# Reordering the weight chunks of a gated linear recurrence, with its decay work cut into steps

## The chip, the cores and the metric

The kernel runs on one core of a Trainium2 chip. The metric is the device time of one execution in microseconds (us). It is a forward pass of a four-layer network over 256 tokens of width 1024 in one launch; the change touches one stage of it, some 140 us long, in the middle of the third layer.

## The reference, cut to what matters

The stage is the mixer of the third layer, a chunked linear recurrence with a forget gate. One product `u @ w_in` gives four groups of 1024 columns: query, forget gate, value and output gate, each for 8 heads of 128.

```python
q_raw, f_raw, v, g = proj[:, :, 0], proj[:, :, 1], proj[:, :, 2], proj[:, :, 3]
log_f = jnp.log(lb + (1.0 - lb) * jax.nn.sigmoid(f_raw))
k = (1.0 - lb) * jax.nn.sigmoid(-f_raw)
q = jax.nn.silu(q_raw)
...
b = jnp.cumsum(log_f, axis=2)                 # within a chunk of tokens
q_dec = q * jnp.exp(b)
k_inv = k * jnp.exp(-b)
...                                           # scores, values, state from chunk to chunk
o = o * lax.rsqrt(jnp.mean(o * o, axis=-1, keepdims=True) + NORM_EPS)
o = o * norm_g.astype(jnp.float32).reshape(H, HG_VDIM)
o = o.reshape(B, S, D_MODEL) * jax.nn.silu(g.reshape(B, S, D_MODEL))
return o.astype(u.dtype) @ w_out
```

## The kernel before, in words

All products with weights are computed from operands that are split into a high and a low part, three products for each. A chunk of weights is 1024 x 256: one DMA of 1 MB into `raw`; ScalarE writes the high part `whi` in two halves of 128 x 1024; VectorE writes the low part `wlo` of the first half. In this stage GpSimd writes the low part of the second half (`pool_lo`). A chunk is then 48 matmuls of 256 columns on TensorE. There are buffers for the split parts of two chunks, so the parts of a chunk are written while the chunk before it is multiplied, and over those of the chunk before that: the first half becomes free when three quarters of that earlier chunk are done, the second half at its end.

The order on TensorE is the order in which the program is written (`manual_schedule` for it alone). ScalarE, VectorE and GpSimd work through orders that a planner sets when the kernel is built: each takes, of what is ready by the planner's own estimates, the instruction that the program names first. On the chip these orders are fixed, and each engine waits for the next instruction in its own order.

The stage, `hgrn`, has 17 chunks of products. Value and gate of head pair 0 come first, together. Then the four forget chunks follow each other; each is followed on ScalarE by an exponential (`he`), and on VectorE by an addition (`hs`), a reciprocal, a product (`kk`) and two scalings (`lf`). When all four are done, ScalarE takes the logarithm of `lf` in one instruction (`self.act(f2, f2, AF.Ln)`), VectorE makes eight scans (`bt`) and one difference (`rl`), ScalarE makes the exponentials of +`rl` and -`rl`, and VectorE makes eight products for `kk`. The rest are the chunks of the four head pairs: query 0; value 1, query 1, gate 1; value 2, query 2, gate 2; value 3, query 3, gate 3.

A head pair's own work, `hgrn_pair`, is a generator. `tick()` advances every generator in the background list by one step, and is called twice in each chunk (once in each of the four groups of 12 matmuls of the output projection that use the first half of the heads). Its steps are: a first empty one (five for pair 0), transposes of `kk` (`phk`), scores (`pha`), chunk states (`phs`, then `hS` on VectorE, a chain of three states), outputs (`pho`) with the normalisation after them (squares `hjunk` on ScalarE, `hss` on VectorE, a power `hF` on GpSimd, `hsg` on VectorE), an empty one, and the transposes `pot` into the operand (`hoh`, `hol`) of the output projection. `settle()` ticks until the named generators have ended. The output projection (`out_proj`, tile `po`) settles everything before its first matmuls with the second half of the heads.

Of the kernel before, what the change touches and what calls it, by code (L numbers as in the profile page):

```python
# [7 lines left out]
F32 = mybir.dt.float32  # L8
# [3 lines left out]
AF = mybir.ActivationFunctionType  # L12
OP = mybir.AluOpType
# [5 lines left out]
KT = 8  # L19
# [71 lines left out]
class Net:  # L91
# [1280 lines left out]
    def hgrn(self, nxt):  # L1372
        nc, tc, i = self.nc, self.tc, self.i
        w = self.w3(i["hgrn_w_in"][0])
        lb, ilb = self.lb, self.ilb
        v3 = lambda x: x.rearrange("p (k t) -> p k t", t=T)
        u, tile = self.next
        self.hold = True
        with self.phase("hgrn", 6) as hp:
            G = self.bcast_row(hp, "G", self.grow[0][0])  # L1380
            self.hmask = hp.tile([128, 128], I32, name="hmask")
            nc.sync.dma_start(self.hmask, i["hmask"])
            reset = hp.tile([128, 256], F32, name="reset")
            nc.sync.dma_start(reset, i["cst3"][:, 64:320])
            out = self.pair("ho")
            v, sg = {}, {}
            c = slice(0, 256)
            pv, pg = self.toks([w[:, :, 2048:3072][:, :, c], w[:, :, 3072:4096][:, :, c]], u, ["phv", "phg"], tile)
            self.hgrn_v(0, v, pv, hp)
            self.hgrn_g(0, sg, pg, hp)  # L1390
            self.pool_lo = True
            kk, lf = v3(self.A("kk")), v3(self.A("lf"))
            for p in range(4):
                ps = self.ws(w[:, :, 1024 + 256 * p:1024 + 256 * (p + 1)], u, "pf")
                e = hp.tile([128, 512], F32, tag="he", name="he", bufs=2)
                s = hp.tile([128, 512], F32, tag="hs", name="hs", bufs=2)
                self.act(e, ps, AF.Exp, scale=-1.0)
                self.ts(s, e, 1.0, None, OP.add)
                nc.vector.reciprocal(s, s)
                self.tt(kk[:, 2 * p:2 * p + 2, :].rearrange("p a b -> p (a b)"), e, s, OP.mult)  # L1400
                for b in range(2):
                    k = 2 * p + b
                    self.ts(lf[:, k, :], s[:, b * T:(b + 1) * T], ilb[:, k:k + 1], lb[:, k:k + 1], OP.mult, OP.add)
            f2 = lf.rearrange("p k t -> p (k t)")
            self.act(f2, f2, AF.Ln)
            bt, rl = self.A("bt"), self.A("rl")
            b3 = v3(bt)
            for k in range(KT):
                nc.vector.tensor_tensor_scan(b3[:, k, :], reset, lf[:, k, :], 0.0, op0=OP.mult, op1=OP.add)
            bc = bt.rearrange("p (c t) -> p c t", t=64)  # L1410
            rc = rl.rearrange("p (c t) -> p c t", t=64)
            self.tt(rc, bc, bc[:, :, 31:32].to_broadcast([128, 32, 64]), OP.subtract)
            E = [hp.tile([128, 8, 3], F32, tag=f"hE{n}", name=f"hE{n}") for n in range(2)]
            self.act(E[0], rl.rearrange("p (k c t) -> p k c t", c=4, t=64)[:, :, 0:3, 63], AF.Exp)
            self.act(E[1], bt.rearrange("p (k c t) -> p k c t", c=4, t=64)[:, :, 1:4, 31], AF.Exp)
            ep = bt
            self.act(f2, rl, AF.Exp, scale=-1.0)
            self.act(ep, rl, AF.Exp)
            for k in range(KT):
                self.stt(kk[:, k, :], kk[:, k, :], ilb[:, k:k + 1], lf[:, k, :])  # L1420
            am = []
            for n in range(2):
                a = hp.tile([128, 4, 128], F32, tag=f"am{n}", name=f"am{n}")
                nc.vector.memset(a, 0.0)
                am.append(a)
            ch = []
            for p in range(4):
                c = slice(256 * p, 256 * (p + 1))
                if p:
                    self.hgrn_v(p, v, self.tok(w[:, :, 2048:3072][:, :, c], u, "phv"), hp)  # L1430
                ps = self.ws(w[:, :, c], u, "phq")
                if p > 1:
                    self.settle(ch[p - 2])
                q = hp.tile([128, 2, T], F32, tag="hq", name="hq", bufs=2)
                q2 = q.rearrange("p a b -> p (a b)")
                self.silu2(q2, ps)
                self.stt(q2, q2, 0.5, v3(ep)[:, 2 * p:2 * p + 2, :].rearrange("p a b -> p (a b)"))
                ch.append(self.hgrn_pair(p, q, v, sg, kk, E, am[p % 2], hp, out))
                self.bg.append(ch[p])
                if p:  # L1440
                    self.hgrn_g(p, sg, self.tok(w[:, :, 3072:4096][:, :, c], u, "phg"), hp)
            self.pool_lo = False
            self.hold = False
            a = self.as_act(*out)
            self.out_norm(self.w3(i["hgrn_w_out"][0]), a, G, nxt)

    def hgrn_v(self, p, v, pv, hp):
        v[p] = hp.tile([128, 2, 2, 128], F32, tag="hv", name="hv", bufs=2)
        self.act(v[p].rearrange("p t h d -> p (t h d)"), pv)

    def hgrn_g(self, p, sg, pg, hp):
        sg[p] = hp.tile([128, 2, 2, 128], F32, tag="hsg", name="hsg", bufs=2)
        self.silu2(sg[p].rearrange("p t h d -> p (t h d)"), pg)

    def hgrn_pair(self, p, q, v, sg, kk, E, am, hp, out):
        nc = self.nc
        H = 2 * p
        v = v[p]
        for _ in range(1 if p else 5):
            yield  # L1460
        pk = self.pss("phk")
        for t in range(2):
            for h in range(2):
# [19 lines left out]
        for n in range(3):  # L1483
# [3 lines left out]
            t, o = n // 2, 64 * (n % 2)  # L1487
# [14 lines left out]
        for t in range(2):  # L1502
            for h in range(2):
                n = 2 * t + h
# [360 lines left out]
```

## Time and profile before

| | us |
|---|---|
| median of 3 runs | 2248.33 |
| lowest, highest | 2245.28, 2248.53 |
| the profiled execution | 2249.15 |
| its span, first to last instruction | 2247.3 |

The span is divided by engine: PE is TensorE's matmuls, PEld its weight loads, DVE VectorE, ACT ScalarE, POOL GpSimd, SP the queue that issues the DMAs. A busy PE isn't PE at its peak, and an idle engine that nothing waits for costs nothing. The stage of the change lies from about 1411 us (norm and first two chunks) to 1567 us of the span; its forget chunks begin at 1428.9 us.

### The profile page before, as it was taken

To read this page: it belongs to the slowest core of one execution; us is meant where nothing else is said; L and a number is where in the kernel's file an instruction comes from. 1 tells how busy PE (TensorE), PEld (TensorE's weight loads), DVE (VectorE), ACT (ScalarE), POOL (GpSimd) and SP (SyncE) were. 2 spreads that over 40 slices of the span, in tenths; PEclk is the share of its full clock that TensorE was granted. 3 is DMA by queue.
4 is the path that set the end of the run, shared out by engine and by line. 5 is a ranking of instruction groups with operands and counts; after the bars stand their busy time and mean duration, and the time that the engine had idled before them with its cause. 6 is when DMAs were issued, how large, how long until landed. Compare 5 with 4: busy or idle time off the path is not lost.

```text
span 2247.3 us, 38710 instructions
## 1 busy us (share of the span) xinstructions
PE 2171.4 (97%) x15635; PEld 2006.1 (89%) x15635; DVE 1683.8 (75%) x2596; ACT 1273.6 (57%) x1992; POOL 163.8 (7%) x142
## 2 busy tenths in 40 slices
PE   8999999999999999999999998989999999999998
PEld 7998998998899999788888886887998899998997
DVE  6879677776587886599999996777787676665554
ACT  5655545445566554487877775655543555555443
POOL 0031100000003210000000000331000000000000
PEclk9999999999999999999999999999999999999999
DMA  7444577876454366689999994434687554444553
GB/s 239 150 134 145 195 243 246 276 267 233 158 169 141 117 224 209 219 311 356 335 317 349 321 345 156 156 121 160 209 290 282 184 183 147 154 150 136 182 181 131
DMA packets 338527, 478.61 MB, mean 213 GB/s; under 512 B 9874, under 2 KB 239116, under 8 KB 338340
## 3 DMA queue, kind: packets, MB, share of 16 engines
q1 hardware_dynamic: 338340, 476.05, 62.7%
q8 instruction: 125, 2.05, 0.4%
q14 instruction: 62, 0.51, 0.1%
HBM read 474.95 MB, written 1.06 MB: 212 GB/s over the span
## 4 chain that ended last, share of the span: by engine, by line
issue 31%; PE 23%; DVE 2%; POOL 1%; ACT 1%; POOLq 0%; DVEq 0%; ACTq 0%
PE peg L176 5%; PE peu L176 5%; PE pey L176 5%; PE pf L176 1%; PE po L176 1%; PE phg L176 1%; DVE wlo L164 1%; PE phq L176 1%; PE pgat L176 1%; PE phv L176 1%; PE pho L176 1%; PE psc L176 0%; PE pht L179 0%; POOL ms L351 0%; POOL rs L182 0%
## 5 line engine op out<-in xcount | busy, mean ns | idle before, releaser
L164 DVE TENSOR_TENSOR wlo<-raw,whi 128x1024 fp32r<-128x1024 f32 (+2 forms) x802 | 930.1, 1180 | 289.2 <-ACT whi L161 281.4
L161 ACT ACTIVATE whi<-raw 128x1024 fp32r<-128x1024 f32 (+3 forms) x828 | 832.3, 1023 | 508.9 <-PE po L176 60.3
L176 PE MATMUL pu<-uh,whi 128*128 128x256 f32 x480 | 134.1, 279 | 0.0
L176 PE MATMUL pg<-uh,whi 128*128 128x256 f32 x480 | 134.0, 279 | 0.0
L176 PE MATMUL pg<-uh,wlo 128*128 128x256 f32 x480 | 133.8, 279 | 0.0
L176 PE MATMUL pg<-ul,whi 128*128 128x256 f32 x480 | 133.8, 279 | 0.0
L176 PE MATMUL pu<-uh,wlo 128*128 128x256 f32 x480 | 133.7, 279 | 0.0
L176 PE MATMUL pu<-ul,whi 128*128 128x256 f32 x480 | 133.7, 279 | 0.0
L173 DVE SCALAR_TENSOR_TENSOR acc<-raw,cond,acc 128x1024 f32<-128x1024 f32 x84 | 107.6, 1281 | 21.7 <-DMA raw<-in_ada_w_dram 20.9
L351 POOL TENSOR_SCALAR ms<-ss 128x1 f32<-128x1 f32 x30 | 15.6, 521 | 1482.9 <-ACT junk L161 1482.9
L176 PE MATMUL paq<-uh,whi 128*128 128x256 f32 x384 | 111.0, 289 | 0.0
L176 PE MATMUL pqkv<-uh,whi 128*128 128x256 f32 x384 | 108.6, 283 | 0.0
L176 PE MATMUL paq<-ul,whi 128*128 128x256 f32 x384 | 107.2, 279 | 0.0
L176 PE MATMUL paq<-uh,wlo 128*128 128x256 f32 x384 | 107.2, 279 | 0.0
L176 PE MATMUL pqkv<-uh,wlo 128*128 128x256 f32 x384 | 107.1, 279 | 0.0
L176 PE MATMUL pqkv<-ul,whi 128*128 128x256 f32 x384 | 107.1, 279 | 0.0
L176 PE MATMUL po<-wlo,fh 128*128 128x512 f32 x264 | 103.1, 390 | 1.5 <-DVE wlo L164 1.5
L176 PE MATMUL po<-whi,fh 128*128 128x512 f32 x264 | 103.2, 391 | 0.5 <-DVE fm L173 0.5
L176 PE MATMUL po<-whi,fl 128*128 128x512 f32 x264 | 102.8, 389 | 0.0
L176 PEld LDWEIGHTS pg<-ul,whi 128*128 128x128 f32 x480 | 91.1, 190 | 0.0
L176 PEld LDWEIGHTS pu<-ul,whi 128*128 128x128 f32 x480 | 90.9, 189 | 0.0
L176 PEld LDWEIGHTS pu<-uh,whi 128*128 128x128 f32 x480 | 90.1, 188 | 0.9 <-ACT whi L161 0.9
(475 smaller groups left out, 6450.0 us busy)
## 6 DMA issues: line engine op xcount, KB each, us to landing
raw<-in_w_in_dram SPq DMA_DIRECT2D x70, 1024.0 KB
raw<-in_ada_w_dram SPq DMA_DIRECT2D x48, 1024.0 KB
raw<-in_ffn_w_in_dram SPq DMA_DIRECT2D x44, 1024.0 KB
raw<-in_attn_w_in_dram SPq DMA_DIRECT2D x36, 1024.0 KB
raw<-in_exp_w_gate_dram SPq DMA_DIRECT2D x32, 1024.0 KB
raw<-in_exp_w_up_dram SPq DMA_DIRECT2D x32, 1024.0 KB
raw<-in_exp_w_down_dram SPq DMA_DIRECT2D x32, 1024.0 KB
raw<-in_ffn_w_out_dram SPq DMA_DIRECT2D x20, 1024.0 KB
```

Source lines behind the costliest of these rows:

```text
L161: self.nc.scalar.activation(out, in_, func, scale=scale, bias=bias, **k)
L164: self.nc.vector.tensor_tensor(out, a, b, op=op)
L173: self.nc.vector.scalar_tensor_tensor(out, a, s, b, op0=op0, op1=op1)
L176: self.nc.tensor.matmul(out, lhsT, rhs, start=start, stop=stop, skip_group_check=skip)
L351: self.nc.gpsimd.tensor_scalar(ms, self.ss[:, t, 0:1], self.ss[:, t, 1:2], EPS, op0=OP.add, op1=OP.add)
```

## The change

The chunks are put in another order: forget 0, value 1, forget 1, gate 1, forget 2, value 2, forget 3, gate 2, value 3, query 0, query 1, gate 3, query 2, query 3. The logarithm, the scans, the differences, the exponentials and the products for `kk` become a generator, `decays`, that is put on the background list after forget 3: it yields after each second scan, after the differences, and after each half of the exponentials. It is settled before query 0. The difference, the two exponentials and the products are done in halves. The buffers for values become four in place of two, those for gates three in place of two. Pair 0 has one empty step, as the others have.

```diff
-            for p in range(4):
-                ps = self.ws(w[:, :, 1024 + 256 * p:1024 + 256 * (p + 1)], u, "pf")
+            cols = lambda off, p: w[:, :, off + 256 * p:off + 256 * (p + 1)]
+
+            def forget(p):
+                ps = self.ws(cols(1024, p), u, "pf")
...
+            values = lambda p: self.hgrn_v(p, v, self.tok(cols(2048, p), u, "phv"), hp)
+            gate = lambda p: self.hgrn_g(p, sg, self.tok(cols(3072, p), u, "phg"), hp)
...
-            self.act(f2, f2, AF.Ln)
-            for k in range(KT):
-                nc.vector.tensor_tensor_scan(b3[:, k, :], reset, lf[:, k, :], 0.0, op0=OP.mult, op1=OP.add)
-            self.tt(rc, bc, bc[:, :, 31:32].to_broadcast([128, 32, 64]), OP.subtract)
-            self.act(f2, rl, AF.Exp, scale=-1.0)
-            self.act(ep, rl, AF.Exp)
-            for k in range(KT):
-                self.stt(kk[:, k, :], kk[:, k, :], ilb[:, k:k + 1], lf[:, k, :])
+            def decays():
+
+                self.act(f2, f2, AF.Ln)
+                for k in range(KT):
+                    nc.vector.tensor_tensor_scan(b3[:, k, :], reset, lf[:, k, :], 0.0, op0=OP.mult, op1=OP.add)
+                    if k % 2:
+                        yield
...
+                for n in range(2):
+                    c = slice(16 * n, 16 * n + 16)
+                    self.tt(rc[:, c], bc[:, c], bc[:, c, 31:32].to_broadcast([128, 16, 64]), OP.subtract)
+                self.act(E[0], rl.rearrange("p (k c t) -> p k c t", c=4, t=64)[:, :, 0:3, 63], AF.Exp)
+                self.act(E[1], bt.rearrange("p (k c t) -> p k c t", c=4, t=64)[:, :, 1:4, 31], AF.Exp)
+                yield
+                for n in range(2):
+                    c = slice(1024 * n, 1024 * n + 1024)
+                    self.act(f2[:, c], rl[:, c], AF.Exp, scale=-1.0)
+                    self.act(ep[:, c], rl[:, c], AF.Exp)
+                    for k in range(4 * n, 4 * n + 4):
+                        self.stt(kk[:, k, :], kk[:, k, :], ilb[:, k:k + 1], lf[:, k, :])
+                    yield
+
             ch = []
-            for p in range(4):
-                c = slice(256 * p, 256 * (p + 1))
-                if p:
-                    self.hgrn_v(p, v, self.tok(w[:, :, 2048:3072][:, :, c], u, "phv"), hp)
-                ps = self.ws(w[:, :, c], u, "phq")
+
+            def query(p):
+                ps = self.ws(cols(0, p), u, "phq")
                 if p > 1:
                     self.settle(ch[p - 2])
...
                 ch.append(self.hgrn_pair(p, q, v, sg, kk, E, am[p % 2], hp, out))
                 self.bg.append(ch[p])
-                if p:
-                    self.hgrn_g(p, sg, self.tok(w[:, :, 3072:4096][:, :, c], u, "phg"), hp)
+
+            forget(0)
+            values(1)
+            forget(1)
+            gate(1)
+            forget(2)
+            values(2)
+            forget(3)
+            dec = decays()
+            self.bg.append(dec)
+            gate(2)
+            values(3)
+            self.settle(dec)
+            query(0)
+            query(1)
+            gate(3)
+            query(2)
+            query(3)
...
-        v[p] = hp.tile([128, 2, 2, 128], F32, tag="hv", name="hv", bufs=2)
+        v[p] = hp.tile([128, 2, 2, 128], F32, tag="hv", name="hv", bufs=4)
...
-        sg[p] = hp.tile([128, 2, 2, 128], F32, tag="hsg", name="hsg", bufs=2)
+        sg[p] = hp.tile([128, 2, 2, 128], F32, tag="hsg", name="hsg", bufs=3)
...
-        for _ in range(1 if p else 5):
-            yield
+        yield
```

## Rows read from the trace of the kernel before

**Rows 1.** The page: busy time of the engines, and memory traffic in 40 slices.

```profile
PE 2171.4 (97%) x15635; PEld 2006.1 (89%) x15635; DVE 1683.8 (75%) x2596; ACT 1273.6 (57%) x1992; POOL 163.8 (7%) x142
...
GB/s 239 150 134 145 195 243 246 276 267 233 158 169 141 117 224 209 219 311 356 335 317 349 321 345 156 156 121 160 209 290 282 184 183 147 154 150 136 182 181 131
```

**Rows 2.** Waits of PE, 1429 to 1570 us: total us, times, longest.

```profile
PE phg L176 <- DVE wlo L164: 5.6, 1, 5.6
...
PE pot L179 <- DVE hsg L173: 0.8, 3, 0.4
```

**Rows 3.** Timeline of PE about the longest wait: start, duration, instruction, idle before.

```profile
1468.75 0.28 PE L176 MATMUL phg<-whi,uh 128*128 128x256 f32 x1
1474.63 0.58 PE L176 MATMUL phg<-wlo,uh 128*128 128x256 f32 x1 [5.60 <-DVE wlo L164]
```

**Rows 4.** Windows: length, busy PE PEld DVE ACT POOL, granted clock, DMA, GB/s.

```profile
1429.00:1570.00 141.00, 131.26 (x1079) 117.61 (x1079) 107.46 (x161) 71.61 (x120) 44.12 (x24) 0.98 0.45 146
...
887.20:889.70 2.50, 0.00 (x0) 0.00 (x0) 1.96 (x3) 0.00 (x0) 0.00 (x0) 1.00 0.00 0
889.70:893.70 4.00, 3.96 (x34) 3.96 (x35) 3.04 (x3) 1.52 (x2) 0.00 (x0) 1.00 0.43 119
1404.90:1408.30 3.40, 0.00 (x0) 0.00 (x0) 2.56 (x5) 3.40 (x7) 1.60 (x2) 0.79 0.00 1
1408.30:1412.30 4.00, 3.92 (x18) 3.92 (x18) 3.03 (x6) 2.38 (x7) 0.00 (x0) 0.50 0.81 261
...
1474.60:1478.60 4.00, 3.97 (x19) 3.98 (x19) 4.00 (x2) 2.82 (x4) 2.90 (x1) 0.51 0.69 214
```

**Rows 5.** Timeline of DVE, the first forget chunk and the scans.

```profile
1444.60 0.73 DVE L170 TENSOR_SCALAR lf<-hs,ilb,lb 128x256 f32<-128x256 f32 x2
...
1466.58 6.87 DVE L1409 TENSOR_TENSOR_SCAN bt<-reset,lf 128x256 f32<-128x256 f32 x8 [1.39 <-ACT lf L161]
1473.38 1.19 DVE L164 TENSOR_TENSOR wlo<-raw,whi 128x1024 fp32r<-128x1024 f32 x1
1474.49 2.28 DVE L164 TENSOR_TENSOR rl<-bt 128x2048 f32<-128x2048 f32 x1
```

**Rows 6.** The tile of the scans: ns min/median/max, first and last start.

```profile
L1409 DVE TENSOR_TENSOR_SCAN bt<-reset,lf x8: 659/668/2773, 1466.6 to 1472.8; 128x256 f32<-128x256 f32 x8
```

**Rows 7.** Timeline of POOL under the scans.

```profile
1469.00 2.75 POOL L262 TENSOR_TENSOR wlo<-raw,whi 128x1024 fp32r<-128x1024 f32 x1 [7.86 <-ACT whi L161]
```

**Rows 8.** The chain that ended last: one chunk of 48 matmuls.

```profile
1506.77 5.66 PE phg L176 x48
```

**Rows 9.** Timeline of ACT, the first forget chunk and the logarithm.

```profile
1434.94 1.06 ACT L161 ACTIVATE whi<-raw 128x1024 fp32r<-128x1024 f32 x1 [0.41 <-PE pf L176]
...
1464.63 1.92 ACT L161 ACTIVATE lf<-lf 128x2048 f32<-128x2048 f32 x1 [4.34 <-DVE lf L170]
```

**Rows 10.** The tile hs of the forget chunks: ns min/median/max, first and last start.

```profile
L168 DVE TENSOR_SCALAR hs<-he x4: 415/422/2243, 1436.5 to 1458.5; 128x512 f32<-128x512 f32 x4
...
L164 DVE TENSOR_TENSOR kk<-he,hs x4: 676/678/2496, 1442.2 to 1463.3; 128x512 f32<-128x512 f32 x4
```

**Rows 11.** Timeline of PE, last pair and output projection.

```profile
1541.74 1.16 PE L176 MATMUL phs<-hv,hkt 64*128 64x128 f32 x12
...
1548.72 0.50 PE L176 MATMUL po<-whi,hoh 128*128 128x512 f32 x1
...
1551.36 0.39 PE L176 MATMUL po<-whi,hol 128*128 128x512 f32 x1
1552.16 0.33 PE L179 MATMUL pot<-cst,hsg 128*128 128x128 f32 x1 [0.41 <-DVE hsg L173]
...
1553.02 0.48 PE L176 MATMUL po<-whi,hoh 128*128 128x512 f32 x1
```

**Rows 12.** Timeline of DVE, the last pair's states and operand.

```profile
1543.54 1.22 DVE L164 TENSOR_TENSOR wlo<-raw,whi 128x1024 fp32r<-128x1024 f32 x1
...
1546.29 0.60 DVE L170 TENSOR_SCALAR hS<-hS,hE,hE 128x128 f32<-128x128 f32 x2
```

More of the change, by code (lines that the diff above doesn't have):

```diff
@@ L1403, in hgrn @@
                     self.ts(lf[:, k, :], s[:, b * T:(b + 1) * T], ilb[:, k:k + 1], lb[:, k:k + 1], OP.mult, OP.add)
+            values = lambda p: self.hgrn_v(p, v, self.tok(cols(2048, p), u, "phv"), hp)
+            gate = lambda p: self.hgrn_g(p, sg, self.tok(cols(3072, p), u, "phg"), hp)
             f2 = lf.rearrange("p k t -> p (k t)")
-            self.act(f2, f2, AF.Ln)
             bt, rl = self.A("bt"), self.A("rl")
             b3 = v3(bt)
-            for k in range(KT):
-                nc.vector.tensor_tensor_scan(b3[:, k, :], reset, lf[:, k, :], 0.0, op0=OP.mult, op1=OP.add)
-            bc = bt.rearrange("p (c t) -> p c t", t=64)
-            rc = rl.rearrange("p (c t) -> p c t", t=64)
-            self.tt(rc, bc, bc[:, :, 31:32].to_broadcast([128, 32, 64]), OP.subtract)
             E = [hp.tile([128, 8, 3], F32, tag=f"hE{n}", name=f"hE{n}") for n in range(2)]
-            self.act(E[0], rl.rearrange("p (k c t) -> p k c t", c=4, t=64)[:, :, 0:3, 63], AF.Exp)
-            self.act(E[1], bt.rearrange("p (k c t) -> p k c t", c=4, t=64)[:, :, 1:4, 31], AF.Exp)
             ep = bt
-            self.act(f2, rl, AF.Exp, scale=-1.0)
-            self.act(ep, rl, AF.Exp)
-            for k in range(KT):
-                self.stt(kk[:, k, :], kk[:, k, :], ilb[:, k:k + 1], lf[:, k, :])
             am = []
@@ L1425, in hgrn @@
                 am.append(a)
-            ch = []
-            for p in range(4):
-                c = slice(256 * p, 256 * (p + 1))
-                if p:
-                    self.hgrn_v(p, v, self.tok(w[:, :, 2048:3072][:, :, c], u, "phv"), hp)
-                ps = self.ws(w[:, :, c], u, "phq")
+            def decays():
[4 more added lines that the diff above has]
+                        yield
+                bc = bt.rearrange("p (c t) -> p c t", t=64)
+                rc = rl.rearrange("p (c t) -> p c t", t=64)
+                for n in range(2):
[11 more added lines that the diff above has]
+                    yield
+            ch = []
+            def query(p):
+                ps = self.ws(cols(0, p), u, "phq")
                 if p > 1:
```

## The prediction

> **What bounds the kernel now.** I read the page first: PE is busy for 97% of the span [rows 1], so an edit is worth what it takes from PE's idle time, or gives to it. Then the window of the stage: of 141.0 us PE is busy for 131.3 [rows 4], so no order of the same products can win more than 9.7 us there, and a half clock somewhat more. The list of PE's waits shows one that counts, 5.6 us of gate 1's matmuls for a low part `wlo` from DVE [rows 2]. The timeline has it at 1468.75 to 1474.63: 5.88 us between two starts that are 0.12 apart in a chunk of 48 in 5.66 us [rows 3, 8], so 5.8 are lost. The next 4 us run at half clock, 1.2 GHz (granted 0.51), and get 19 matmuls done that take 2.2 us at full clock: 1.8 more [rows 4, 8]. That is **7.6 us, 0.34%**, and it is what the change can reach. DVE's timeline shows why: the logarithm ends at 1466.55 [rows 9], all eight scans become ready at once, stand ahead of the low part in program order, and run as a block of 6.87 us; the low part follows at 1473.38 [rows 5]. One scan of the eight takes 2.77 us where the others take 0.67 [rows 6]: it starts while POOL writes a low part, 1469.00 to 1471.75 [rows 7]. So POOL holds DVE up, for some 2.1 us.
>
> **What leaves, what stays.** No matmul, DMA or split is added. The 13 chunks in the new order are the same 13 MB; one per 5.66 us is 185 GB/s, and the page has slices over 340 [rows 1, 8], so their order on the DMA queue costs nothing. The third gate buffer makes gate 3's last step wait for pair 0's `pot`; only pair 3's normalisation, some 20 us later, reads it: nothing.
>
> **The forget chunks apart.** In before each forget chunk gives DVE about as much as PE needs time for it, and DVE falls behind. With value and gate chunks between, DVE has two chunks' time for each, and starts forget 3's work at once. I count from forget 3's last matmul as 0. For the first forget chunk in before, whose work DVE also found itself free for, that matmul is at 1434.94 (ACT's split of the next weights is released by it), and `lf` ends at 1445.33 [rows 5, 9]: 10.4 us. In these are two holds by POOL: `hs` 2.24 in place of 0.42, `kk` 2.50 in place of 0.68 [rows 10], 1.8 each. So `lf` of forget 3 ends between 6.8 and 10.4. The split of value 3's second half comes just before `he`, as there, so that the first hold comes back; the second needs POOL's next low part to fall on `kk`. I take 9.5. The logarithm of 1.92 [rows 9] then ends at **11.4** (8.7 to 12.3).
>
> **The steps between products.** Gate 2 and value 3 last until 2 x 5.66 = 11.3. The ticks put scans 0 to 3 into gate 2 and 4 to 7 into value 3, but ticks order the program, not DVE: no scan can start before the logarithm has ended, and by then both chunks are multiplied. So the scans run as one block again, under query 0, and the low part that meets them is **query 1's**. Behind the logarithm on ACT queue value 3's copy and the splits for query 1; query 1's low part comes after scans and differences in program order. Its end: 11.4 + 6.87 (scans with one hold) + 2.28 (differences) + 1.19 (itself), less 0.1 of overlaps [rows 5] = 21.6. PE needs it at 3 x 5.66 + 0.1 = 17.1. It waits **4.5 us**, and I count the half clock of 1.8 after it as in before. Bounds: 8.7 + 8.1 without a hold is 16.8, no wait; 12.3 + 10.2 + 2.1 for a second hold is 24.6, a wait of 7.5. In sum this part gives 4.5 + 1.8 - 7.6 = **-1.3** (-7.6 to +1.7).
>
> **The end of the stage.** Gate 3 now comes before query 2, so nothing follows query 3. In before its chunk gave pair 3 two ticks. Now the four ticks of the output projection are spent on the empty step, `phk`, `pha` and `phs`, and `pho`, the empty step and `pot` all fall into `settle()`, with no product between. In before `pho` ended at 1548.72, 12 matmuls of the projection followed until 1551.59, `pot` began at 1552.16 and the projection went on at 1553.02 [rows 11]. These 4.30 us are the normalisation's way through ACT, DVE, POOL and DVE. The 12 matmuls covered 2.87 of it; `pot` itself is some 0.45 (0.86 from its first start to the projection's, less its waits for `hsg`); idle were 1.0. Without the cover 3.85 are idle: +2.9. The chain of states took from 1541.74 to 1546.89 [rows 11, 12], 5.15 with one low part of 1.22 in it. It was hidden by 12 matmuls; now only `phs` (1.16), pair 2's `pot` and three quarters of pair 3's `pho` are there, 1.16 + 0.45 + 2.2 = 3.8, so 0.1 to 1.35 show; I take 0.3. The clock: after a break of over 3.4 us PE was granted 0.50 in the next 4 us, after one of over 2.5 still 1.00 [rows 4]. 3.85 is nearer to the first: 1.8, with nothing as the bound. Sum **+5.0** (+2.9 to +6.1).
>
> **Pairs 0 and 1** no longer run their `pho` back to back. Both now have other steps between normalisation and `pot`; of the 0.8 us of waits for `hsg` [rows 2] I take off 0.5 (0 to 0.8).
>
> **Sum:** -1.3 + 5.0 - 0.5 = **+3.2 us** on the profiled execution's 2249.15, which is 0.8 above the median of the runs, so 2251.5 for the median. What a measurement of this kernel can tell from no change is about 0.2%, 4.5 us: I forecast **no change that can be told**, leaning to slower.
>
> **Rivals.**
>
> *The low part gets in front* (faster or nearly so). At 1473.38 DVE did gate 1's low part between the last scan and the difference [rows 5], as the difference was waiting for the scan. If query 1's does likewise and `lf` comes unheld, it ends at 8.7 + 6.8 + 1.2 = 16.7, PE doesn't wait, and all 7.6 are won: -7.6 + 5.0 - 0.5 = -3.1, 2245.2; with the clock kept at the end, 2243.4. Against it: the first difference needs only the first four scans now, is ready when the last one ends, and goes first by program order. Chance 0.22.
>
> *A second hold.* By POOL's hold, each low part that POOL writes under the block of scans and differences costs DVE 2.1; query 1's second half falls there too when query 0's does. 4.5 becomes 6.6, the time 2253.6. For it: `hs`, `kk` and a scan were all held by what POOL did; against it: POOL's next low part came after the scans in before. The Trainium skill (SBUF — State Buffer, section "SBUF: two separate sides") has VectorE and GpSimd share a pair of ports that one locks for a whole instruction, while the other is fully blocked; by that rule every such low part would cost a hold, and the trace agrees where it shows one (2.77 against 0.67). Chance 0.15.
>
> *The wait moves to query 0* (slower). If query 0's first low part isn't done before the logarithm ends, it stands behind scans and differences and ends at 21.6, where PE needs it at 11.4: a wait of 10.2 + 1.8, so 12.0 - 7.6 + 5.0 - 0.5 = +8.9, 2257.2. It decides whether DVE takes it in the 1.9 us in which it waits for the logarithm. Its split can start at three quarters of gate 2, 4.3, well before `lf` is done at 9.5; so I give it 0.13.
>
> That the change doesn't do what it says is in the forecast itself: the steps spread nothing. What it would take for them to: a logarithm done before value 3.
>
> **Chances.** Forecast 0.45, second hold 0.15, query 0 0.13, in front 0.22, something that these rows don't show 0.05. Slower by over 0.2% (above 2252.8): query 0, most of the second hold, the upper end of the forecast, 0.32. Faster (below 2243.8): the larger part of "in front", and the rest, 0.20. Same: 0.48. The range takes in both outer cases, 2242.5 to 2258.
>
> **What would show it.** Eight scans without a gap under query 0; PE's longest wait of the stage at query 1's second matmul, with a low part of DVE as releaser; after pair 3's `pho` nearly 4 us without a matmul, and a granted clock near 0.5 in the projection after it. I am wrong if query 1 starts on time, if a low part stands between the scans or ahead of the differences, or if matmuls of the projection still run between pair 3's `pho` and `pot`.

## The result, and the profile after

The changed kernel takes **2264.58 us** (median of 12 runs, 2259.18 to 2274.42) where the kernel before, run beside it, takes 2248.85 (12 runs): a ratio of **1.0064, 95% interval 1.0047 to 1.008**. It is slower by 0.64%, some 14 us; the prediction was 2251.5 with a range up to 2258. The profiled execution's span went from 2247.3 to 2258.4 us.

To compare traces I measure the stage in each: from the first forget matmul of the chain of waits to the start of the last matmul ahead of the wait for `uh` that follows the output projection. Before, that is 1429.10 to 1567.32, **138.2 us**; after, 1430.19 to 1581.94 (the last of the three matmuls in the first row below), **151.8 us**. So the stage lost 13.5 us. The rest of the network, which the change doesn't touch, took 2.4 us less in this execution than in that of before, and is left alone here. Timeline of PE in the kernel after:

```profile
1581.71 0.50 PE L176 MATMUL pn<-diag,h 128*128 128x128 f32 x3
1583.78 0.38 PE L176 MATMUL pg<-whi,uh 128*128 128x256 f32 x1 [1.57 <-ACT uh L161]
```

The waits of PE in the stage after, 1430 to 1582 us (total us, times, longest), where before had one that counts [rows 2]:

```profile
PE phq L176 <- DVE wlo L164: 5.8, 2, 4.8
PE pho L176 <- DVE hS L170: 4.3, 4, 1.4
PE pot L179 <- DVE hsg L173: 3.5, 1, 3.5
PE phv L176 <- DVE wlo L164: 0.9, 1, 0.9
PE phg L176 <- DVE wlo L164: 0.8, 2, 0.4
```

Four groups of waits, in four places. The first two are in VectorE's timeline:

```profile
1443.75 2.86 DVE L170 TENSOR_SCALAR lf<-hs,ilb,lb 128x256 f32<-128x256 f32 x2
1446.53 2.35 DVE L164 TENSOR_TENSOR wlo<-raw,whi 128x1024 fp32r<-128x1024 f32 x2
1448.80 2.61 DVE L168 TENSOR_SCALAR hs<-he 128x512 f32<-128x512 f32 x1
1451.44 3.35 DVE L1401 RECIPROCAL hs<-hs 128x512 f32<-128x512 f32 x1
...
1482.79 1.21 DVE L164 TENSOR_TENSOR wlo<-raw,whi 128x1024 fp32r<-128x1024 f32 x1
1484.25 6.91 DVE L1424 TENSOR_TENSOR_SCAN bt<-reset,lf 128x256 f32<-128x256 f32 x8 [0.25 <-ACT lf L161]
1491.09 2.33 DVE L164 TENSOR_TENSOR rl<-bt 128x1024 f32<-128x1024 f32 x2
1493.34 1.21 DVE L164 TENSOR_TENSOR wlo<-raw,whi 128x1024 fp32r<-128x1024 f32 x1
```

and in GpSimd's, which writes low parts:

```profile
1443.23 2.90 POOL L262 TENSOR_TENSOR wlo<-raw,whi 128x1024 fp32r<-128x1024 f32 x1 [3.80 <-ACT whi L161]
1448.34 2.79 POOL L262 TENSOR_TENSOR wlo<-raw,whi 128x1024 fp32r<-128x1024 f32 x1 [2.21 <-ACT whi L161]
```

Read them together. `lf` starts 0.5 us after GpSimd's low part and takes 2.86 for two where two took 0.73 [rows 5]; `hs` starts 0.5 after the next one and takes 2.61 in place of 0.42 [rows 10]. This happens in each of the four forget chunks, eight low parts of GpSimd and eight holds, and VectorE has no room left: the windows below show it busy, holds included, for 23.96 of 24.10 us. PE then waits for low parts at gate 1, value 2, gate 2 and query 0. After that the eight scans stand in one block, as before [rows 5], the differences behind them, and query 1's low part ends at 1494.55. The rows are length, busy PE, PEld, DVE, ACT, POOL, granted clock, DMA share, GB/s; the last three are the half clock after query 1's wait, after the waits at query 2, and in the projection:

```profile
1441.60:1465.70 24.10, 22.75 (x194) 22.33 (x194) 23.96 (x16) 10.44 (x12) 11.69 (x4) 1.00 0.56 178
...
1494.60:1498.60 4.00, 3.99 (x18) 3.99 (x19) 3.97 (x10) 4.00 (x5) 0.00 (x0) 0.50 0.72 218
...
1526.50:1530.50 4.00, 3.99 (x17) 3.10 (x18) 2.82 (x5) 1.47 (x8) 0.03 (x1) 0.50 0.31 78
...
1566.50:1570.50 4.00, 3.96 (x12) 3.25 (x12) 1.26 (x4) 0.95 (x2) 0.00 (x0) 0.50 0.00 0
```

The other two groups are in PE's timeline, at the finishing of pair 0 behind query 2 (first fence) and of pairs 2 and 3 ahead of the projection (second):

```profile
1519.88 1.16 PE L176 MATMUL phs<-hv,hkt 64*128 64x128 f32 x12
1520.97 0.66 PE L179 MATMUL pot<-cst,hsg 128*128 128x128 f32 x4
1522.50 0.49 PE L176 MATMUL pho<-hv,am 128*128 128x128 f32 x2 [0.88 <-DVE hS L170]
...
1526.51 0.69 PE L176 MATMUL pho<-hS,hq 128*64 128x128 f32 x2 [1.41 <-DVE hS L170]
```

```profile
1555.01 1.16 PE L176 MATMUL phs<-hv,hkt 64*128 64x128 f32 x12
...
1557.76 0.49 PE L176 MATMUL pho<-hv,am 128*128 128x128 f32 x2 [1.01 <-DVE hS L170]
...
1561.36 0.43 PE L176 MATMUL pho<-hS,hq 128*64 128x128 f32 x2 [1.05 <-DVE hS L170]
...
1566.07 1.42 PE L179 MATMUL pot<-cst,hsg 128*128 128x128 f32 x4 [3.50 <-DVE hsg L173]
...
1580.19 2.02 PE L176 MATMUL pn<-diag,h 128*128 128x128 f32 x16 [0.27 <-DVE diag L168]
```

`settle()` ticks every generator, not only the one that it names. Behind query 2 it is there to finish pair 0, but pair 1's states (`phs`) have just run and its outputs (`pho`) come with the next tick, with nothing between but pair 0's `pot`. So the chain of three states is on PE's path, and query 3's 48 matmuls follow at half clock, 7.80 us in place of 5.66 [rows 8]:

```profile
1526.51 2.04 PE pho L176 x8
1528.55 7.80 PE phq L176 x48
...
1566.59 0.90 PE pot L179 x3
1567.49 12.44 PE po L176 x48
```

(chain of waits of after: start, us, what).

### The profile page after: what moved, and what is told of

The parts are those of the page before. It is cut to its first block, busy times and chain, and to the rows that moved or that the text cites. A ratio compares the mean times of both kernels' runs of the same rounds, so it can differ in the third digit from the quotient of the medians.

```text
span 2258.4 us, 38704 instructions
## 1 busy us (share of the span) xinstructions
PE 2174.3 (96%) x15635; PEld 2007.3 (89%) x15635; DVE 1697.6 (75%) x2597; ACT 1275.3 (56%) x1994; POOL 166.0 (7%) x142
## 4 chain that ended last, share of the span: by engine, by line
issue 31%; PE 22%; DVE 3%; POOL 1%; ACT 1%; POOLq 0%; DVEq 0%; ACTq 0%
PE peg L176 5%; PE peu L176 5%; PE pey L176 5%; PE po L176 1%; PE pf L176 1%; PE phq L176 1%; DVE wlo L164 1%; PE pgat L176 1%; PE phg L176 1%; PE phv L176 1%; PE psc L176 0%; PE pht L179 0%; POOL ms L351 0%; PE pho L176 0%; POOL rs L182 0%
## 5 line engine op out<-in xcount | busy, mean ns | idle before, releaser
L176 PEld LDWEIGHTS pg<-uh,whi 128*128 128x128 f32 x480 | 90.4, 188 | 0.9 <-ACT fh L161 0.9
```

Of the source, the lines that this page charges most:

```text
L176: self.nc.tensor.matmul(out, lhsT, rhs, start=start, stop=stop, skip_group_check=skip)
```

## The experiments

Each time is given as the ratio to the kernel before on the same chip with its interval, and as the stage's length in the trace; the two agree within 3 us in every run (a ratio of 1.0010 is 2.25 us). A stage's length is that of one execution. How far it moves from one execution of a kernel to the next no run shows, and half clock after the same breaks, which came in some traces and not in others (last section), is worth up to 3.0 us of it. So a difference of some 3 us or less between two stages is told below as the traces have it, and is not shown by them alone. Each ratio is from 12 runs of the kernel named, but from 11 for e1 and e11 and 6 for e10.

A first finding is in the programs as they are built: written with the decays as one block ahead of gate 2, without steps, the changed kernel has the same instructions in the same order on all five engines. The steps by themselves change nothing.

| run | ratio (95%) | stage, us |
|---|---|---|
| changed kernel | 1.0064 (1.0047 to 1.0080) | 151.8 |
| e1 low part of query 1 on GpSimd | 1.0047 (1.0025 to 1.0070) | 149.1 |
| e2 three sets of pair buffers | 1.0026 (1.0007 to 1.0045) | 145.4 |
| e3 as e2, gate 3 last | 1.0025 (1.0003 to 1.0046) | 142.9 |
| e4 no low parts by GpSimd | 1.0033 (1.0014 to 1.0053) | 145.7 |
| e5 e3 and e4 | 1.0023 (1.0008 to 1.0038) | 140.6 |
| e6 logarithm in four | 1.0053 (1.0035 to 1.0070) | 150.7 |
| e7 before, no low parts by GpSimd | 0.9996 (0.9980 to 1.0013) | 136.2 |
| e8 before, logarithm takes the scaling | 0.9993 (0.9977 to 1.0008) | 137.1 |
| e9 before, tanh | 0.9999 (0.9987 to 1.0010) | 137.0 |
| e10 changed, tanh | 1.0065 (1.0045 to 1.0084) | 150.8 |
| e11 e3, tanh | 1.0026 (1.0010 to 1.0042) | 143.9 |
| e12 before, tanh, logarithm in four | 0.9988 (0.9968 to 1.0007) | 133.6 |
| e13 changed, tanh, logarithm in four | 1.0028 (1.0013 to 1.0043) | 147.3 |
| e14 e3, tanh, logarithm in four | 1.0000 (0.9982 to 1.0017) | 136.7 |
| e15 e12, no low parts by GpSimd | **0.9969 (0.9954 to 0.9985)** | 131.6 |

### Is each loss where the trace shows it?

**e1.** In `query(1)` alone, GpSimd writes the first half's low part too:

```diff
-            if self.pool_lo and k0:
+            if self.pool_lo and (k0 or self.pool_first):
```

> The changed kernel with one instruction moved: the low part of the first half of query 1's weights is written by GpSimd and not by VectorE, where it stands behind eight scans and two differences. In the changed kernel PE stands 5.1 us between two matmuls of query 1 for it, and the other 46 of the chunk take 7.62 us where a chunk of 48 takes 5.66. Theory A, each loss has its own place and this one is worth its wait and its half clock, 5.0 + 2.1 = 7: nearly all of it comes back, the time is 6 to 7 us below the changed kernel's, some 8 us above before, though the scans and differences end about 2 us later by one more hold of GpSimd. Rival B, VectorE is late as a whole, and whatever needs it next takes the wait over (the products for kk, which the first transposes of pair 0 need, or the low part of gate 3): less than 2.5 us come back and a new wait of PE stands within 12 us of the old place.

2.7 us of the stage came back: rival B, nearly to its number (by the ratios the intervals overlap). Query 1 starts on time, but the scans take 9.09 us with two holds, and ScalarE's exponentials, which wait for them, stand ahead of gate 3's high part in its order: gate 3 waits 2.9 us for `whi` and 1.4 for a low part, the longest of three:

```profile
PE phg L176 <- ACT whi L161: 2.9, 1, 2.9
PE phg L176 <- DVE wlo L164: 2.8, 3, 1.4
```

**e2.** Three sets of `hq`, `hS` and `am`, so that query 2 needn't finish pair 0:

```diff
-                if p > 1:
-                    self.settle(ch[p - 2])
+                if p > 2:
+                    self.settle(ch[p - 3])
...
             query(3)
+            self.settle(ch[1])
```

> The changed kernel with three sets of the buffers of a pair (hq, hS, am) in place of two, so that query 2 does not have to finish pair 0 and query 3 not pair 1; pair 1 is finished after query 3. In the changed kernel finishing pair 0 at query 2 runs pair 1's states and outputs back to back on PE, with no product between: two waits of 1.15 and 1.68 us, and the 48 matmuls of query 3 after them in 7.80 us in place of 5.66. Theory A, it is the missing product between states and outputs: these 4.6 us come back, and as finishing pair 1 brings pairs 2 and 3 one step forward, the two waits of 1.28 and 1.33 us at the end as well, so the time is 5 to 7 us below the changed kernel's, some 8 to 9 us above before; the last wait of 3.77 stays. Rival B, VectorE is late there by its own work (low parts and copies in front of the states), so that the outputs wait wherever they stand: less than 2 us come back, and PE's waits for hS stay near 4 us in sum.

Theory A: the stage is 6.3 us shorter, and the ratio's interval lies below the changed kernel's. Of the waits of `pho` for states, 4.3 us in the changed kernel, 0.8 are left; the last wait of `pot` stays.

```profile
PE phq L176 <- DVE wlo L164: 5.8, 2, 4.8
PE pot L179 <- DVE hsg L173: 4.8, 3, 3.9
PE phg L176 <- DVE wlo L164: 1.1, 2, 0.7
PE pho L176 <- DVE hS L170: 0.8, 1, 0.8
```

**e3.** The same three sets without the last line of e2 (pair 1 is finished by the output projection), and `gate(3)` behind `query(3)`.

> As the kernel with three sets of pair buffers, and gate 3's chunk goes behind query 3, where it stood before the change, so that pair 3 has two more steps inside products. Theory A, the end of the stage cost what it lost in cover: the break of 3.77 us between pair 3's outputs and its transposes shrinks to under 1.2 us, and the output projection's 48 matmuls after it take near 11 us and not 12.4: 4 to 5 us below the kernel with three sets, some 4 us above before. In the middle, where gate 3 is gone, pair 0 is finished at query 3 with one step less of cover, which may give back up to 1.5 us at pair 1. Rival B, the end is set by something other than the order (the weights of the projection, or VectorE), and the break stays over 3 us.

The end behaved as theory A has it: no wait of `pot` over 0.54 us, and 40 matmuls of the projection in 9.73 us, where the changed kernel took 12.44 for 48. But the stage gained only 2.6 on e2, since at query 3, where pair 0 is finished now, two breaks of 1.15 and 0.41 us and 20 `pho` in 4.25 us (2.94 at full clock) came in. The ratio can't tell e3 from e2.

**e4.** `self.pool_lo = True` is moved to just ahead of `query(0)`.

> The changed kernel with GpSimd writing no low part from forget 0 to value 3; VectorE writes them, nine more of some 1.15 us. In the changed kernel each of the four forget chunks shows hs at 2.2 to 2.6 us and one of two lf at some 2.1 in place of 0.42 and 0.73, each under a low part of GpSimd; VectorE is busy for 23.96 of the 24.1 us of forget 1 to forget 3 and PE waits 0.6, 1.1 and 1.2 us for low parts there. Theory A, the holds fill VectorE: without them hs and lf fall to 0.42 and 0.7, which takes some 3.5 us from each forget chunk and adds 2.3, the three short waits shrink to under 1 us in sum, and lf of forget 3 ends 1 to 3 us sooner after its last matmul, so that query 1's wait of 5 falls by as much: 3 to 6 us below the changed kernel's, some 10 us above before. Rival B, the long hs and lf have another cause than GpSimd and stay: VectorE has 10 us more to do, the three waits grow by 2 us and more each, and the kernel is 4 us or more slower than the changed one.

Theory A. `hs` is back at 0.42 in all four chunks (tile `hs`: ns min/median/max), the short waits are gone, and the stage is 6.1 us shorter. But 3.0 of these are pair 1's `pho` and query 3's chunk, which ran at full clock here behind the same two breaks; that this part is GpSimd's doing is not shown.

```profile
L170 DVE TENSOR_SCALAR lf<-hs,ilb,lb x8: 399/409/2481, 1446.0 to 1481.7; 128x256 f32<-128x256 f32 x8
L168 DVE TENSOR_SCALAR hs<-he x4: 419/420/422, 1440.6 to 1473.9; 128x512 f32<-128x512 f32 x4
```

One part of A failed: query 1's wait did not shrink, it grew from 5.1 to 6.2 us between two matmuls. PE, with no wait at query 0, came 1.2 us sooner; `lf` of forget 3 came only 0.6 sooner (10.5 us after the chunk's last matmul), as one of its two was held for 2.48 by the first low part that GpSimd wrote again, and the scans behind it took 6.90 as ever.

**e5.** e3 and e4 in one.

> Three edits together: three sets of pair buffers, gate 3 behind query 3, and no low part by GpSimd from forget 0 to value 3. With the first two the stage, from the first forget matmul to the last of the output projection, took 142.9 us in the profile (changed kernel 151.8, before 138.2). Theory A, the losses lie in separate places and add up: without GpSimd's holds the three short waits before query 1 (0.6, 1.0 and 1.2 us) go and query 1's wait grows by some 1 us, as the third edit alone showed, so 141 us, 2 to 3 us above before. Rival B, the third edit's 6 us came off the whole length, and all of it adds: 137 us, 1 to 2 us below before. Rival C, the losses overlap and nothing is added to 142.9.

Theory A, 140.6 for 141: the waits lie in separate places and both go. The gains don't simply add, 8.9 of e3 and 6.1 of e4 against 11.2 here; 3.0 of the 3.8 between are the half clock that e4 was spared, behind breaks that e3 doesn't have. Query 1's wait, 5.9 us, is about as long as gate 1's was before (5.6); what is left over before are the breaks at query 3.

### Why does the wait ahead of query 1 survive?

**e6.** One line of the changed kernel:

```diff
-                self.act(f2, f2, AF.Ln)
+                for n in range(4):
+                    self.act(f2[:, 512 * n:512 * n + 512], f2[:, 512 * n:512 * n + 512], AF.Ln)
```

> The changed kernel with one line else: the logarithm is taken in four pieces of two heads each, so that the scans of two heads wait for their own forget chunk and not for forget 3. Theory A, the decays came as one block because one logarithm over all heads stood before them: with four, two scans stand behind the last logarithm and six lie in the forget chunks; query 1's wait of 5.1 us and the half clock after it (2.1) go, while VectorE, full already in the forget chunks, makes PE wait 1 us more in two or three of them: 3 to 5 us below the changed kernel's, some 10 us above before. Rival B, VectorE has the same work before query 1 in either form, and what it is late by comes out of PE all the same, only in other places: within 2 us of the changed kernel. Rival C, ScalarE's six more table loads, 1.28 us each, make the high parts late: PE waits for whi, and the kernel is slower than the changed one.

Rival B: 1.1 us of the stage. The scans of the first six heads now do lie in the forget chunks, and PE waits for query 0 and 1 in four pieces instead of two, 5.6 us in sum where the changed kernel has 5.8 (waits 1430 to 1582):

```profile
PE phq L176 <- POOL wlo L262: 3.6, 2, 1.9
...
PE phq L176 <- DVE wlo L164: 1.5, 1, 1.5
```

The fourth piece, 0.5 us, is for a high part.

**e7.** The kernel before without GpSimd's low parts until the scans are named.

> The kernel before with no low part by GpSimd until the scans are named; VectorE writes four more, 4.6 us. Theory A, what a low part of GpSimd costs VectorE hangs on the instruction that it meets: in the forget chunks of before only two were held (hs of forget 0, kk of forget 0, 1.8 us each), the other low parts of GpSimd lie under reciprocals, which took 3.35 us each time. So without them VectorE has 4.6 more and 3.6 less to do, gate 1's wait stays at 5 to 8 us, and the time is 0 to 3 us above before. Rival B, GpSimd holds VectorE in every low part, seen or not: as in the changed kernel its absence is worth 3 us and more, and the time is 3 us or more below before.

Nearer to theory A: nothing that the ratio can tell, and the trace's stage 2.0 us shorter, outside both numbers. The wait stands at value 1 now, 4.5 us. That GpSimd cost the kernel before little is seen in its timelines of POOL and DVE: this low part lies inside a reciprocal, and neither is longer for it.

```profile
1447.38 2.40 POOL L262 TENSOR_TENSOR wlo<-raw,whi 128x1024 fp32r<-128x1024 f32 x1 [3.25 <-ACT whi L161]
```

```profile
1446.83 3.35 DVE L1399 RECIPROCAL hs<-hs 128x512 f32<-128x512 f32 x1
```

**e8.** The scalings `lf` go into the logarithm, one piece for each head, in the kernel before (the reciprocal then writes into `lf`):

```diff
...
-                for b in range(2):
-                    k = 2 * p + b
-                    self.ts(lf[:, k, :], s[:, b * T:(b + 1) * T], ilb[:, k:k + 1], lb[:, k:k + 1], OP.mult, OP.add)
...
-            self.act(f2, f2, AF.Ln)
+            for k in range(KT):
+                self.act(lf[:, k, :], lf[:, k, :], AF.Ln, scale=ilb[:, k:k + 1], bias=lb[:, k:k + 1])
```

> The kernel before, its order of chunks unchanged; the eight scalings lf on VectorE go into the logarithm's own scale and bias, in eight pieces of one head. Theory A, gate 1's wait (5.8 us, and 1.8 us of half clock after it) came from one logarithm and eight scans in a block behind it; with pieces the scans of the first heads lie in the forget chunks, VectorE has 3.3 us less to do, and at most two scans are left behind forget 3: the wait falls under 1.5 us and the time is 5 to 7 us below before. Rival B, the order of the chunks is what is needed: VectorE has no room in four forget chunks in a row, falls behind by what it takes in there, and the wait only moves to the first chunk that needs a low part: less than 2 us below before. Rival C, six more table loads of 1.28 us on ScalarE make the high parts late, and it is slower than before.

Rival B: 1.2 us of the stage, and nothing by the ratio. Gate 1's wait went, and five breaks of 0.8 to 2.7 us came, most of them for low parts of VectorE.

**e9, e10, e11.** VectorE's work is cut and nothing is moved: `sigmoid(-x) = 0.5 - 0.5 tanh(x/2)`, in the kernel before (e9), the changed one (e10), and e3 (e11).

```diff
-                self.act(e, ps, AF.Exp, scale=-1.0)
-                self.ts(s, e, 1.0, None, OP.add)
-                nc.vector.reciprocal(s, s)
-                self.tt(kk[:, 2 * p:2 * p + 2, :].rearrange("p a b -> p (a b)"), e, s, OP.mult)
+                self.act(e, ps, AF.Tanh, scale=0.5)
+                self.ts(kk[:, 2 * p:2 * p + 2, :].rearrange("p a b -> p (a b)"), e, -0.5, 0.5, OP.mult, OP.add)
...
-                    self.ts(lf[:, k, :], s[:, b * T:(b + 1) * T], ilb[:, k:k + 1], lb[:, k:k + 1], OP.mult, OP.add)
+                    self.ts(lf[:, k, :], e[:, b * T:(b + 1) * T], ilh[:, k:k + 1], lbh[:, k:k + 1], OP.mult, OP.add)
```

> The kernel before with VectorE's work in the forget chunks cut and nothing moved: the sigmoid comes from one hyperbolic tangent on ScalarE, so that in each forget chunk the addition (0.42 us), the reciprocal (3.35) and the product (0.68) on VectorE become one scaling of 0.42; the logarithm stays one, the chunks stay in their order. 16 us of VectorE's work go ahead of gate 1. Theory A, what PE waits for between the forget chunks and gate 1 is VectorE's total, not the order of anything: with 16 us less the scans are done before gate 1's low part is due, its wait of 5.8 us and the 1.8 us of half clock go, and no other wait over 1 us comes in its place: 6 to 8 us below before, 0.3%. Rival B, it is the one logarithm behind which everything queues: the block still stands in front of some low part or of a high part behind the exponentials, and 3 us or more of waits stay, at query 1 or value 1: less than 4 us below before.

> The changed kernel with the same cut of VectorE's work in the forget chunks, 16 us. Theory A, VectorE's total sets the waits up to query 1: the three short ones (0.6, 1.1, 1.2) and query 1's 5.0 with 2.1 of half clock go, and the losses behind them (finishing pair 0 at query 2, and the end of the stage) stay as they are, since they are PE's order and not VectorE's load: 9 to 10 us below the changed kernel's, 4 to 5 us above before. Rival B, the losses behind query 1 are VectorE's lateness too, and go with it: within 2 us of before or below it. Rival C, query 1's wait is that of the block behind one logarithm and stays over 3 us: 8 us or more above before.

> The changed order with three sets of pair buffers, gate 3 behind query 3, and VectorE's work in the forget chunks cut by 16 us as in the two kernels beside it. Theory A, everything found so far is taken away but the 2 to 3 us at query 3, where pair 0 is finished: the stage takes 133 to 135 us (before 138.2), 3 to 5 us below before, and the order of before with the same cut is 2 to 3 us better still. Rival B, with VectorE free the alternating order shows what it is worth, and it beats the order of before with the same cut by 2 us or more. Rival C, some of query 1's wait stays, and it is not below before.

My theory fell, three times. With 16 us less work VectorE is idle for a third of the forget chunks in e9 (busy for 14.98 of 22.50 us), and PE waits as long: in e9 3.2 us at query 1 and 3.1 at gate 1, in e10 and e11 7.8 at query 0. VectorE's timeline in e10 shows the reason:

```profile
1476.17 6.88 DVE L1424 TENSOR_TENSOR_SCAN bt<-reset,lf 128x256 f32<-128x256 f32 x8 [1.99 <-ACT lf L161]
1482.97 1.19 DVE L164 TENSOR_TENSOR rl<-bt 128x1024 f32<-128x1024 f32 x1
...
1485.82 1.66 DVE L173 SCALAR_TENSOR_TENSOR kk<-kk,ilb,lf 128x256 f32<-128x256 f32 x4
1487.41 1.21 DVE L164 TENSOR_TENSOR wlo<-raw,whi 128x1024 fp32r<-128x1024 f32 x1
```

The block starts earlier, so it meets an earlier chunk. From the first scan to the low part are 11.2 us, and ScalarE, which has the logarithm ahead of that chunk's high part, gives VectorE the high part only at 1477.1. PE needs the low part at 1480.7.

### Both at once

e12 is e9 with e6's line, e13 is e10 with it and e14 is e11 with it; e15 is e12 without GpSimd's low parts up to query 0, as in e7.

> The kernel before with both: VectorE's work in the forget chunks cut by 16 us (sigmoid from one hyperbolic tangent), and the logarithm in four pieces of two heads. Each alone won nothing that can be told, and waits of some 7 us with their half clock stayed in each. Theory A, it is the length of what stands ahead of a low part in VectorE's fixed order, against the one chunk of lead that two sets of split buffers give: the cut alone left a block of scans and differences of 9 to 11 us, the pieces alone left a full VectorE; with both, two scans and one difference (3.6 us, 5.7 with a hold) are left behind the last logarithm, less than a chunk: waits of low parts under 1.5 us in sum, the time 5 to 7 us below before. Rival B, ScalarE is the next to be late: eight table loads of 1.28 us and its own fixed order put high parts behind logarithms and exponentials, PE waits for whi, and less than 2 us is won. Rival C, waits of PE in this stretch do not come from the block at all, and stay near 7 us.

> The changed kernel with the same two edits. Theory A, as in the kernel before with both: nothing over 1.5 us is left of the waits up to query 1 (10 us of the changed kernel with the half clock), and what is left is PE's order behind it, finishing pair 0 at query 2 (4.7) and the end of the stage (6 to 7): 4 to 6 us above before, and 10 us above the kernel before with both edits. Rival B, what stays of the loss shrinks with VectorE's load as well: within 2 us of before. Rival C, the waits up to query 1 stay over 4 us: 8 us or more above before.

> The changed order with every loss that was found taken away: three sets of pair buffers, gate 3 behind query 3, VectorE's work cut, the logarithm in four. Theory A, only 3 us at query 3, where pair 0 is finished, are left: the stage takes 133 to 135 us (before 138.2), 3 to 5 us below before. Rival B, a wait of the same kind appears in a new place, as in every single edit so far, and it is not below before.

> The kernel before with both edits and no low part by GpSimd up to query 0. With the cut alone VectorE was held in each forget chunk (kk 2.24 us in place of 0.42), but had several us of idle time there. Theory A, the holds cost nothing once VectorE has room: within 1 us of the kernel with both edits. Rival B, a hold in the short chain of the last forget chunk (kk, lf, logarithm, scans) makes the whole chain 1.8 us late, which is what a low part waits for: 1 to 2 us below it.

With a short block and room on VectorE the wait falls from 5.6 us to 2.1 in e12 and 1.2 in e15, whose longest waits of PE in the stage are these:

```profile
PE phq L176 <- DVE wlo L164: 1.2, 1, 1.2
PE pot L179 <- DVE hsg L173: 0.8, 3, 0.4
PE po L176 <- DVE hol L173: 0.5, 1, 0.5
```

Theory A of e12 is right in kind and short in size, a wait of 2.1 where it had under 1.5 and a stage 4.6 us shorter where it had 5 to 7; by the ratio e12 is no change that can be told. Two scans and the whole difference are still ahead of query 1's low part, and that low part is itself held, 2.96 us for 1.2. e15 comes out 2.0 us below e12 in the trace, rival B's number, but by the ratios their intervals overlap, so that B is not shown. **e15 beats both kernels: 0.31% below before, and by the two ratios 0.9% below the changed one.** e13 loses 13.7 us to e12 in the trace with the same two edits, about what the changed kernel loses to before, and 9 by the ratios; its waits up to query 1 are 2.7 us in sum, between theory A and rival C. e14, the changed order with all that was found mended, stands level with before, and not below it as theory A had it: query 0 still waits 2.8 us for a low part of GpSimd and a high part, and query 3's breaks stay.

## Why the prediction was wrong

The signs that I had named all showed: eight scans without a gap under query 0, the longest wait of a low part at query 1, near 4 us without a matmul ahead of pair 3's `pot`, a granted clock of 0.50 in the projection after it. The time was still 13 us off, 10 by the traces, as most of the losses that I had no term for showed in none of these signs. By steps, predicted against the stages of the two traces:

| step | predicted | measured |
|---|---|---|
| steps between products: query 1 for gate 1 | -1.3 | -0.4 |
| forget chunks apart | 0 | +3.3 |
| pairs 0 and 1 | -0.5 | +4.5 |
| end of the stage | +5.0 | +6.7 |
| not placed | | -0.6 |
| sum | +3.2 | +13.5 |

**Steps between products: right in the mechanism, near in the number by luck.** Wait 5.0 for 4.5, half clock 2.2 for 1.8 (46 matmuls in 7.62 us), against the 7.6 that went. Counted from forget 3's last matmul query 1's low part ended at 23.3, not 21.6, but PE, itself late by the waits at gate 2 and query 0, came for it at 18.4, not 17.1. The steps spread nothing; e6 shows the reason that I had given, one logarithm, and that removing it alone isn't enough.

**The forget chunks apart: wrong.** "DVE has two chunks' time for each, and starts forget 3's work at once" took the first forget chunk of before as the pattern, but only for the path of forget 3; I put no price on what the pattern does in forget 1 and 2. With two chunks' time GpSimd writes two low parts into each forget chunk's work, and both are held up against VectorE: `lf` of forget 3 ended 11.0 us after its last matmul (1471.24 to 1482.28), not 9.5 and over the bound of 10.4, and the late low parts cost 0.6 at gate 1, 1.1 at value 2, 0.5 at gate 2 and 1.2 at query 0, each break less the 0.12 of a matmul. e4 takes them all away. Query 0's low part was done in the gap ahead of the scans, as I had it, but late.

**Pairs 0 and 1: the step that failed most.** I looked at normalisation and `pot` and took 0.5 off. `settle(ch[0])` at query 2 had one more chunk to cover it in before; with the new order and one empty step for pair 0 it falls right behind pair 1's states. Two breaks, 1.0 and 1.6, `pho` and query 3 at half clock, 0.9 and 2.1, are 5.6 in sum (the 3.0 of half clock came in five of the six traces that have these breaks, last section); the 0.8 that `phs` waited for states in before goes, and 0.3 of waits for `hsg`. e2, where query 2 finishes nothing, gets it back.

**The end of the stage: the right place, the size too small.** From pair 3's first `phs` to the end of the projection the changed kernel takes 25.2 us (1555.01 to 1580.19, both shown above). Before takes 23.8, from the `phs` of [rows 11] to here:

```profile
1565.57 2.02 PE L176 MATMUL pn<-diag,h 128*128 128x128 f32 x16 [0.27 <-DVE diag L168]
```

In these are 24 matmuls of the projection, 5.7 us, that the changed kernel has behind it by then; pair 2's `pot`, 0.4, isn't in them, as it came earlier there. So 6.7 us were lost, over my bound of 6.1. The term that was far off is the chain of states: it showed 2.4 where I took 0.3 and bounded it by 1.35. It is the loss of query 2 again, states and outputs in one `settle()` with nothing but a `pot` between. `pot` waited 3.65 where I had 3.85. Half clock after it cost 1.2 in the projection (47 steps from matmul to matmul in 12.4 us, where 39 took 9.3 before), and `pot` itself took 1.07 for 0.45: 1.8 in sum, the size that I had given the clock. The two breaks of before, 1.4, go off. In e3 and e5, with gate 3 last, the end is back to two such breaks.

**The rivals.** The low part did not get in front. The second hold came in e1 only. "The wait moves to query 0" came in e10 and e11.

**Not placed** are -0.6 us, the sum of small differences. Chunks of 48 without a break took 5.4 to 5.9 us in before and 5.4 to 5.7 after, at a granted clock of 1.00; no run shows why.

**What the change could reach** I put at 7.6 us. e15 takes 6.6 in the trace, without the new order.

**The counts.** The stage has 16 chunks of the input product, not 17, and 14 of them, not 13, stand in the new order; no term of the sum hangs on it.

## What to carry to other kernels

A wait that comes from a block in an engine's fixed order doesn't shrink when the block starts earlier or the engine has less to do elsewhere: it meets another chunk. Cut the block until it is shorter than the lead that the buffers give, and make room, both: either alone moved the wait here and won nothing that could be told, both cut it from 5.6 us to 2.1, and only with GpSimd's low parts taken out as well, which alone won nothing either (e7), was the time clear of before's.

When work is spread over products by ticks, write down for each product which step of which generator falls into it, for `settle()` too; two steps that depend on each other through another engine need a product between them.

A list of signs tests the terms that a prediction has. Ask as well which engines have no slack left in each stretch, and what an unpriced wait there would look like.

## What the runs showed of the hardware

What a low part of GpSimd costs VectorE hangs on what it meets. `hs` and `lf` (one input), `kk`, the scans and low parts (two inputs) were held until it ended, 1.8 to 2.3 us each, and the eight scans of before, 6.87 us with a hold, took 4.77 in e7 without one. The reciprocal took 3.3 to 3.4 us in every run that has it, with a low part inside it or not, and so the kernel before paid for two of the five in its forget chunks, the changed one for all eight. By the Trainium skill (SBUF — State Buffer, section "SBUF: two separate sides") only VectorE's instructions in a two-port mode, or with two SBUF inputs, take part in the lock. The trace agrees as far as it goes: the reciprocal has one input, and went free; that `hs` and `lf`, with one input too, ran in such a mode, no run here shows. The prediction had left that condition out.

The clock doesn't follow from the breaks alone. The same two breaks behind query 2 were followed by a granted clock of 0.50 in the changed kernel (above) and of 1.00 in e4:

```profile
1526.50:1530.50 4.00, 4.00 (x34) 3.54 (x35) 3.64 (x5) 1.47 (x8) 0.97 (x1) 1.00 0.38 92
```

Of the six traces with these two breaks e4's is the only one with full clock behind them: e1, e6, e10 and e13 show 0.50 to 0.58 in the 4 us from the end of the second break, as the changed kernel does, and query 3's chunk took 6.7 to 7.7 us from its first matmul to its last, in e4 5.4. In e9 a break of 3.47 us was followed by 0.60, one of 3.37 by 1.00. So half clock after a break of these lengths can only be given as a chance here, at 1.2 to 3.0 us a time. What decides it stays open.
